# Moving the start addresses of three groups of SBUF tiles in a two-layer decoder trunk

## The chip, the cores and the metric

The kernel runs on one core of one Trainium2 chip. The metric is the device time of one execution in microseconds (us). Times of one instruction are in nanoseconds (ns); the matrix engine's clock is given in cycles where the granted clock is 1.00, its full 2.4 GHz.

## The reference, cut to what matters

The reference computes a decoder trunk of two layers on 256 tokens of width 1024, in float32. Each layer is a sum of residual steps:

```python
h = h + 0.5 * swiglu(rms_norm(h), w_gate, w_up, w_down)        # D_FF = 2816
u = rms_norm(h)
... = split_last(u @ w_in, IN_SIZES)                           # 8616 columns
h = h + (sum_i sigmoid(gate_i) * (y_i @ w_branch_i)) @ w_out   # four token mixers y_i
h = h + cross_attention(rms_norm(h), rms_norm(mem), wq, wk, wv, wo)
h = h + 0.5 * swiglu(rms_norm(h), ...)
```

and a last RMSNorm. Nearly all arithmetic is in the products of 256 tokens with weights that are read once from HBM.

## The kernel before, in words

**Three products for one.** A float32 operand is split into a high part, rounded to the matrix engine's `float32r` type, and a low part, the rest. A product is the sum of three matmuls: high by high, low by high, high by low. For weights, `fetch` does this: a DMA of up to 1 MB brings a chunk of 2048 columns into a `wr` tile, ScalarE writes the high part to a `wh` tile (L341), VectorE the rest to a `wl` tile (L342). Each of the three names has three buffers. For activations, `split` does it (L355, L356).

**Two forms of product.** TensorE first loads a stationary operand of 128 columns (LDWEIGHTS, the engine PEld of the profile) and then streams a moving operand through it (MATMUL, the engine PE). The load for the next matmul begins while the present one streams.

- `linear` (L372): the activations are stationary, 128 tokens of one 128-row block, and 512 columns of the weights move. A chunk of weights serves 24 such matmuls: two token blocks, three products, four row blocks.
- `linear_t` (L390): the weights are stationary and the 256 tokens of the activations move. A chunk serves 48.

The order of TensorE's instructions is the order of the program. Small jobs between them (transposes, attention scores) are generators that `tick` advances at fixed points.

**Where the operands come from.** The normalised residual stream, or the merged branches, lie transposed in four tiles of the pool `xp`: `xh0` and `xl0` (high and low part of the first 512 of the 1024 features) and `xh1`, `xl1` (the second 512). The class `Transposed` fills them, half by half. They are called the halves here. All other activations that meet weights (`hid` of the FFN's down projection, the mixers' outputs `y..`, the memory `mm..`, the cross attention's `xo..`, its keys `xk..`) lie in tiles of 4096 bytes of the pool `mp`. Scratch tiles of 2048 bytes (`toks`, the tag `f`, the gates) lie in the pool `fp`, between `xp` and `sp`; `sp` holds many small tiles and stands ahead of `mp`.

**Where a tile begins.** The pools stand one behind the other in a partition: `cp`, `wr`, `wh`, `wl`, `xp`, `fp`, `sp`, `mp`; within a pool, tags follow in the order of their first use, each rounded up to 32 bytes. Tiles named `gap` only take room. Sizes in the code give these starts, counted within a line of 512 bytes: the buffers of `wr`, `wh`, `wl` at 480, all four halves at 480, all tiles of `fp` at 480, all tiles of `mp` at 480. Steps within a tile from one operand to the next (512, 1024 or 2048 bytes) don't change that. Three cases differ: the weights of most `linear_t` products are written 48 elements later into their buffers (`HELD = 48`, 192 bytes), so that they begin at 160; the projection `wmisc` has 424 columns, so that its row blocks begin at 480, 128, 288 and 448 in turn; and the MLA up projections (L913) have 384, 256 and 512 columns, all beginning at 480.

**The rope tables.** `tables`, a generator, computes angles (`ang`, `angk`, `angc`, 48 elements each, two buffers each in `sp`) with some 20 short VectorE instructions during the first FFN.

Of the kernel before, what the change touches and what calls it, by code (L numbers as in the profile page):

```python
# [11 lines left out]
F32 = mybir.dt.float32  # L12
F32R = mybir.dt.float32r
# [6 lines left out]
P = 128  # L20
L = 2
D = 1024
S = 256
# [66 lines left out]
def _thresholds():  # L90
    out = list(range(1, 17))
    for k in range(1, 16):
        out.append(math.ceil(16 * 8 ** (k / 16) - 1e-9))
    return out
# [55 lines left out]
def program(tc, a, out, upto="all"):  # L150
# [4 lines left out]
    def sb(name, bufs):  # L155
        return ctx.enter_context(tc.tile_pool(name=name, bufs=bufs))
# [5 lines left out]
    xp = sb("xp", 1)  # L162
    fp = sb("fp", 2)
    sp = sb("sp", 4)
# [3 lines left out]
    ctx.enter_context(tc.manual_schedule(engines={mybir.EngineType.PE}))  # L168


    sp.tile([P, 48], F32, tag="gap", name="gap", bufs=1)

    def bank(name):
        return aux.tile([P, 512], F32, tag="aux", name=name)
# [1 line left out]
    def m4(name, dtype=F32):  # L176
        return mp.tile([P, 1024], dtype, tag="m", name=name)
# [7 lines left out]
    def f2(name, tag="f", bufs=5):  # L185
        return fp.tile([P, 512], F32, tag=tag, name=name, bufs=bufs)

    def half(name):
        return f2(name, "half", 2).rearrange("p (k t) -> p k t", k=4)

    def small(name, n):
        return sp.tile([P, n], F32, tag=name, name=name, bufs=2 if n <= 64 else 1)
# [16 lines left out]
    def C(name):  # L209
        o, n = CO[name]  # L210
        return cst[:, o - P:o - P + n]
# [5 lines left out]
    def bcol(l, name):  # L217
        o, n = BO[name]
        return bcs[:, l * NBC + o:l * NBC + o + n]
# [133 lines left out]
    def split(hi, lo, src):  # L353

        act.activation(hi, src, AF.Copy)  # L355
        dve.tensor_tensor(lo, src, hi.bitcast(F32), ALU.subtract)  # L356
# [40 lines left out]
    def transpose4(src, n=4):  # L397

        ps = bank("tr")
        for k in range(n):  # L400
            pe.transpose(ps[:, k * P:(k + 1) * P], src[:, k * P:(k + 1) * P], ident)  # L401
        return ps[:, :n * P].rearrange("p (k t) -> p k t", k=n)

    def split_gain(hi, lo, ps, gain, n=4):

        t = f2("sgt")[:, :n * P].rearrange("p (k t) -> p k t", k=n)
        dve.tensor_tensor(t, ps, gain.unsqueeze(2).to_broadcast([P, n, P]), ALU.mult)
        split(hi[:, :n], lo[:, :n], t)

    def blk(b):  # L410
        return slice(b * P, (b + 1) * P)

    def rstd_of(ss, n, m, name):

        t = small("rs" + name, m)
        r = small(name, m)
        dve.tensor_scalar(t, ss, 1.0 / n, EPS, ALU.mult, ALU.add)
        pool.tensor_tensor(r, t, mhalf[:, :m], ALU.pow)
        return r

    def square_sum(src, out_):
        j = fp.tile([P, 512], mybir.dt.bfloat16, tag="junk", name="junk", bufs=1)
        act.activation(j[:, :src.free_size()], src, AF.Square, accum_out=out_)  # L423

    class Transposed:
# [12 lines left out]
        def half(self, c, wait):  # L438
            yield wait
            hi = xp.tile([P, 4, S], F32R, tag=f"xh{c}", name=f"xh{c}")  # L440
            lo = xp.tile([P, 4, S], F32R, tag=f"xl{c}", name=f"xl{c}")
            for b in range(NB):
                ps = transpose4(self.src(b, c))
                if self.gain is None:
                    split(hi[:, :, blk(b)], lo[:, :, blk(b)], ps)
                else:
                    split_gain(hi[:, :, blk(b)], lo[:, :, blk(b)], ps, self.gain[:, c * 4:(c + 1) * 4])
            self.tiles[c] = (hi, lo)
            if self.name is not None:
                yield 1 if now > 8 else 6  # L450
                with tc.issue_after(last.ins) if now < 20 else ExitStack():
                    for b in range(NB):
                        square_sum(self.src(b, c), self.ss[:, 2 * c + b:2 * c + b + 1])
                if c:
                    s2 = small("ss2", NB)
                    dve.tensor_tensor(s2, self.ss[:, 0:2], self.ss[:, 2:4], ALU.add)
                    self.rstd = rstd_of(s2, D, NB, self.name)
# [73 lines left out]
    def tables():  # L531
        yield 10
        pos = m4("pos").bitcast(I32)
        posi, reli = pos[:, :NB + S], pos[:, 512:896]
        with tc.issue_after(last.ins):
            act.dma_start(posi, a["pos"])
            act.dma_start(cst, a["consts"][:, P:CO["dec"][0]])
            act.dma_start(bcs, a["bcols"])
        act.activation(sel, C("sel")[:16], AF.Copy)
        yield 4  # L540
        for o, b, n in ((0, 0, 128), (128, 1, 256)):
            pool.tensor_tensor(reli[:, o:o + n], posi[:, b:b + 1].to_broadcast([P, n]), posi[:, NB:NB + n], ALU.subtract)
        dve.tensor_copy(relt, reli)
        yield 2
        posf = small("posf", NB)
        dve.tensor_copy(posf, posi[:, :NB])
        twopi = 2 * math.pi
        c1 = 6.28125
        c2 = float(np.float32(np.round((twopi - c1) * 2 ** 21) / 2 ** 21))
        c3 = float(np.float32(twopi - c1 - c2))  # L550
        magic = 1.5 * 2 ** 23
        for b in range(NB):
            ang = small("ang", 48)
            k = small("angk", 48)
            dve.tensor_scalar(ang, C("inv"), posf[:, b:b + 1], None, ALU.mult)
            dve.tensor_scalar(k, ang, 1.0 / twopi, magic, ALU.mult, ALU.add)
            dve.tensor_scalar(k, k, magic, None, ALU.subtract)
            for c in (c1, c2, c3):
                dve.scalar_tensor_tensor(ang, k, -c, ang, ALU.mult, ALU.add)
            co = small("angc", 48)  # L560
            dve.tensor_scalar(co, ang, math.pi / 2, None, ALU.add)
            dve.tensor_scalar(k, co, math.pi, -twopi, ALU.is_gt, ALU.mult)
            dve.tensor_tensor(co, co, k, ALU.add)
            lim = 3.1415925
            dve.tensor_scalar(co, co, lim, -lim, ALU.min, ALU.max)
            dve.tensor_scalar(ang, ang, lim, -lim, ALU.min, ALU.max)
            for o, n, f in ((0, 32, 0), (96, 16, 32)):
                act.activation(tab[:, b, o:o + n], co[:, f:f + n], AF.Sin)
                act.activation(tab[:, b, o + n:o + 2 * n], ang[:, f:f + n], AF.Sin)
                dve.tensor_scalar(tab[:, b, o + 2 * n:o + 3 * n], tab[:, b, o + n:o + 2 * n], -1.0, None, ALU.mult)  # L570
            yield 2

        for l in range(L):
            lp = bcol(l, "lam").rearrange("p (i e d) -> p i e d", i=2, e=2)
            pr = f2("lp")[:, :128].rearrange("p (i d) -> p i d", i=2)
            dve.tensor_tensor(pr, lp[:, :, 0], lp[:, :, 1], ALU.mult)
            s2 = small("ls", 2)
            dve.tensor_reduce(s2, pr, AX.X, ALU.add)
            e2 = small("le", 2)
            act.activation(e2, s2, AF.Exp)  # L580
            li = 0.8 - 0.6 * math.exp(-0.3 * l)
            dve.tensor_tensor(nlam[:, l:l + 1], e2[:, 1:2], e2[:, 0:1], ALU.subtract)
            dve.tensor_scalar(nlam[:, l:l + 1], nlam[:, l:l + 1], li, None, ALU.subtract)

        rel = relt
        rb = bcs[:, L * NBC:].rearrange("p (h k) -> p h k", h=H)
        d8 = sp.tile([P, H, BUCKETS], F32, tag="d8", name="d8", bufs=1)
        dve.tensor_scalar(d8[:, :, 0], rb[:, :, 0], 8.0, None, ALU.mult)
        dve.tensor_tensor(d8[:, :, 1:], rb[:, :, 1:], rb[:, :, :BUCKETS - 1], ALU.subtract)
        dve.tensor_scalar(d8[:, :, 1:], d8[:, :, 1:], 8.0, None, ALU.mult)  # L590
        for hd in range(H):
            dve.tensor_copy(bias[:, hd, 0:128], C("dmask")[:, 128:256])
            dve.tensor_copy(bias[:, hd, 128:384], C("dmask"))
            dve.tensor_scalar(bias[:, hd], bias[:, hd], d8[:, hd, 0:1], None, ALU.add)
        for i, t in enumerate(_thresholds()):
            yield 3

            while 60 <= now < 72:
                yield 1
            ge = (f2("ge", "gate", 4) if now < 60 else f2("ge", "toks", 3))[:, :384]  # L600
            with tc.high_priority(-2000), tc.issue_after(paced.ins):
                dve.tensor_scalar(ge, rel, float(t), None, ALU.is_ge)
                for hd in range(H):
                    dve.scalar_tensor_tensor(bias[:, hd], ge, d8[:, hd, i + 1:i + 2], bias[:, hd], ALU.mult, ALU.add)  # L604
        mark("bias")
# [636 lines left out]
```

## Time and profile before

| | |
|---|---|
| median of three runs | 1589.47 us (1588.9 to 1590.79) |
| the profiled execution | 1589.41 us |
| its span, first to last instruction | 1587.5 us, 20810 instructions |
| TensorE busy (PE) | 1573.3 us, 99% |
| weight loads (PEld) | 1347.7 us, beside PE |
| VectorE, ScalarE | 1067.1 us (67%), 825.6 us (52%) |
| DMA | 281.58 MB, 177 GB/s in the mean |

PE counts the moving of operands, PEld the loading of stationary ones. The duration that the profile gives a matmul contains the way through the array and overlaps the next matmul's; what a matmul costs in a stream is the distance from its start to the next one's start, called its pitch here. It is read from the view of the chain in order of time, where a piece of one line with its length and count gives length by count.

### The profile page before, as it was taken

The page shows a single profiled execution, that of the slowest core. Times are in us where ns is not written, and L with a number is a line of the kernel's source. Part 1 is how long each engine was busy: PE and PEld are TensorE (multiplying, and loading weights), DVE is VectorE, ACT ScalarE, POOL GpSimd, SP SyncE. Part 2 cuts the span into 40 slices and gives each one's busy share as a digit, 9 for nine tenths or more (in the row PEclk, how much of TensorE's full clock was granted, in tenths as well). Part 3 has the DMA queues.
Part 4 walks back from the last instruction along what each step waited for, and adds up shares of the span by engine and source line. Part 5 has one row for each costly group of instructions (what it writes and reads, how often), then busy time and mean ns, then how long its engine had stood idle before and what let it go on. Part 6 is the DMA issues. An engine that isn't in the chain of part 4 may idle for free.

```text
span 1587.5 us, 20810 instructions
## 1 busy us (share of the span) xinstructions
PE 1573.3 (99%) x8236; PEld 1347.7 (85%) x8236; DVE 1067.1 (67%) x1698; ACT 825.6 (52%) x1221; POOL 28.0 (2%) x39
## 2 busy tenths in 40 slices
PE   8999999999999999999999999999999999999998
PEld 6888889898888988888888888898988899888886
DVE  6687699997777666554465546697657766565544
ACT  6544446656654545444454444475575554554443
POOL 0000000000000000000000000000000000000000
PEclk9999999999999999999999999999999999999999
DMA  7655554444555544555555556444546554455552
GB/s 290 204 174 193 188 174 160 158 163 150 209 185 167 182 157 162 185 185 175 192 191 185 186 174 211 150 153 161 184 151 207 186 182 164 156 178 179 191 175 76
DMA packets 41713, 281.58 MB, mean 177 GB/s; under 512 B 4624, under 2 KB 5008, under 8 KB 9488
## 3 DMA queue, kind: packets, MB, share of 16 engines
q1 hardware_dynamic: 39600, 275.07, 51.2%
q10 hardware_dynamic: 2016, 5.19, 1.0%
q8 instruction: 64, 1.05, 0.3%
q14 instruction: 33, 0.27, 0.0%
HBM read 279.20 MB, written 1.05 MB: 177 GB/s over the span
## 4 chain that ended last, share of the span: by engine, by line
PE 98%; ACT 0%; DMA 0%; issue 0%; DVE 0%; SPq 0%; POOLq 0%; POOL 0%
PE lin L372 78%; PE lin L390 11%; PE tr L401 2%; PE ht L507 1%; PE xo L1148 1%; PE xs L1102 1%; PE up L913 1%; PE my L829 0%; PE ds L998 0%; DMA h<-x 0%; PE ms L949 0%; PE pt L640 0%; ACT wh L341 0%; PE my L831 0%; PE do L1021 0%
## 5 line engine op out<-in xcount | busy, mean ns | idle before, releaser
L342 DVE TENSOR_TENSOR wl<-wr,wh 128x1024 fp32r<-128x1024 f32 (+2 forms) x534 | 625.3, 1196 | 383.5 <-ACT wh L341 381.2
L341 ACT ACTIVATE wh<-wr 128x1024 fp32r<-128x1024 f32 (+2 forms) x534 | 533.4, 1033 | 504.7 <-PE lin L372 382.9
L372 PE MATMUL lin<-wh,xh 128*128 128x512 f32 (+1 forms) x1216 | 333.7, 396 | 0.2 <-ACT wh L341 0.2
L372 PE MATMUL lin<-wh,xl 128*128 128x512 f32 (+1 forms) x1216 | 325.4, 389 | 0.0
L372 PE MATMUL lin<-wl,xh 128*128 128x512 f32 (+1 forms) x1216 | 324.6, 389 | 0.0
L372 PEld LDWEIGHTS lin<-wh,xl 128*128 128x128 f32 x1216 | 228.8, 188 | 47.7
L372 PEld LDWEIGHTS lin<-wl,xh 128*128 128x128 f32 x1216 | 228.4, 188 | 47.4
L372 PEld LDWEIGHTS lin<-wh,xh 128*128 128x128 f32 x1216 | 222.5, 189 | 43.1 <-ACT wh L341 1.2
L372 PE MATMUL lin<-wh,hid 128*128 128x512 f32 x704 | 176.0, 390 | 0.0
L372 PEld LDWEIGHTS lin<-wh,hid 128*128 128x128 f32 x704 | 131.6, 188 | 27.1
L372 PE MATMUL lin<-wl,hid 128*128 128x512 f32 x352 | 95.4, 389 | 0.0
L372 PEld LDWEIGHTS lin<-wl,hid 128*128 128x128 f32 x352 | 66.1, 188 | 13.8
L517 ACT ACTIVATE sg<-lin,rffn 128x256 f32<-128x256 f32 x88 | 40.9, 464 | 62.9 <-PE lin L372 62.8
L604 DVE SCALAR_TENSOR_TENSOR bias<-ge,d,bias 128x384 f32<-128x384 f32 x124 | 69.7, 616 | 0.3
L390 PE MATMUL lin<-xh,wh 128*128 128x256 f32 x384 | 62.0, 283 | 0.0
L390 PE MATMUL lin<-xh,wl 128*128 128x256 f32 x384 | 60.5, 279 | 0.0
L390 PE MATMUL lin<-xl,wh 128*128 128x256 f32 x384 | 60.5, 279 | 0.0
L518 DVE SCALAR_TENSOR_TENSOR toks<-lin,rffn,sg 128x256 f32<-128x256 f32 x88 | 42.3, 481 | 25.1 <-ACT sg L517 25.1
L390 PEld LDWEIGHTS lin<-xh,wh 128*128 128x128 f32 x384 | 52.0, 188 | 0.3
L390 PEld LDWEIGHTS lin<-xl,wh 128*128 128x128 f32 x384 | 51.7, 188 | 0.0
L390 PEld LDWEIGHTS lin<-xh,wl 128*128 128x128 f32 x384 | 51.7, 188 | 0.0
L423 ACT ACTIVATE junk<-h 128x512 bf16<-128x512 f32 x36 | 22.4, 622 | 30.5 <-DVE h L491 16.9
(385 smaller groups left out, 1537.0 us busy)
## 6 DMA issues: line engine op xcount, KB each, us to landing
wr<-gu SPq DMA_DIRECT2D x87, 1024.0 KB, 5.1
wr<-win SPq DMA_DIRECT2D x68, 1024.0 KB, 5.1
wr<-dn SPq DMA_DIRECT2D x40, 1024.0 KB, 4.9
wr<-wbr SPq DMA_DIRECT2D x16, 1024.0 KB, 4.9
wr<-w_out SPq DMA_DIRECT2D x8, 1024.0 KB, 5.0
wr<-xa_wk SPq DMA_DIRECT2D x8, 1024.0 KB, 5.0
wr<-xa_wq SPq DMA_DIRECT2D x8, 1024.0 KB, 5.0
wr<-xa_wv SPq DMA_DIRECT2D x8, 1024.0 KB, 5.0
```

What stands on the lines that cost most here:

```text
L341: last = act.activation(hi[:, s], r[:, s], AF.Copy)
L342: dve.tensor_tensor(lo[:, s], r[:, s], hi[:, s].bitcast(F32), ALU.subtract)
L372: pe.matmul(p_[b][:, :n], lhsT=xT(part, k0 + k)[:, b * P:(b + 1) * P], rhs=w[:, k * n:(k + 1) * n], start=first, stop=last)
L390: pe.matmul(ps[i][:, j * 256:(j + 1) * 256], lhsT=ws[w][:, o:o + P], rhs=xT(part, k0 + k), start=k0 + k + part + w + j == 0, stop=k0 + k = ...
L401: pe.transpose(ps[:, k * P:(k + 1) * P], src[:, k * P:(k + 1) * P], ident)
L423: act.activation(j[:, :src.free_size()], src, AF.Square, accum_out=out_)
L507: pe.transpose(ps[:, k, blk(b)], toks[:, b, k * P:(k + 1) * P], ident)
L517: act.activation(sg, ps[:, :256], AF.Silu, scale=xT.r[:, b:b + 1])
L518: paced = dve.scalar_tensor_tensor(toks[:, b], ps[:, 256:], xT.r[:, b:b + 1], sg, ALU.mult, ALU.mult)
L604: dve.scalar_tensor_tensor(bias[:, hd], ge, d8[:, hd, i + 1:i + 2], bias[:, hd], ALU.mult, ALU.add)
L913: pe.matmul(ps[:, :n], lhsT=lowT[p_][:, k0 + k, blk(b)], rhs=wm[w][:, o + k * n:o + (k + 1) * n], start=i == 0, stop=i == len(seq) - 1)
L1102: pe.matmul(ps[:, j], lhsT=q[part][:, 2 * j + k, blk(b)], rhs=kT[c][w][:, 2 * j + k], start=not part + w + k, stop=w + k == 2)
```

## The change: what it does

A gap of 112 elements (448 bytes) is put ahead of the halves in `xp`; the low part of the first half is made 32 elements (128 bytes) longer than it needs; the gap at the head of `sp` grows from 48 to 128 elements (192 to 512 bytes). To make room, the angles lose their six tiles of 192 bytes in `sp` and are taken as three slices of one 2048-byte tile of the tag `f`.

```diff
-    sp.tile([P, 48], F32, tag="gap", name="gap", bufs=1)
+    xp.tile([P, 112], F32, tag="gap", name="gap")
+    sp.tile([P, 128], F32, tag="gap", name="gap", bufs=1)
@@ Transposed.half
             hi = xp.tile([P, 4, S], F32R, tag=f"xh{c}", name=f"xh{c}")
-            lo = xp.tile([P, 4, S], F32R, tag=f"xl{c}", name=f"xl{c}")
+            lo = xp.tile([P, 4 * S + (0 if c else 32)], F32R, tag=f"xl{c}", name=f"xl{c}")
+            lo = lo[:, :4 * S].rearrange("p (k t) -> p k t", k=4)
@@ tables
         for b in range(NB):
-            ang = small("ang", 48)
-            k = small("angk", 48)
+            angs = f2("ang")
+            ang, k, co = (angs[:, i * 48:(i + 1) * 48] for i in range(3))
...
-            co = small("angc", 48)
```

No instruction is added, removed or reordered in the program. In bytes: 480 + 448 = 928, so `xh0` and `xl0` begin at 416 of a 512-byte line; 128 bytes more bring `xh1` and `xl1` to 544, that is 32; `fp` follows at 32. `sp`'s tiles before `mp` shift by 448 + 128 + 320 - 1152 = -256 bytes in all, so `mp` begins at 224. The weights stay at 480, or 160 with `HELD`.

The start of the stationary operand less that of the moving one, within 512 bytes, becomes:

| product | before | after |
|---|---|---|
| `linear` on the first half | 0 | -64 |
| `linear` on the second half | 0 | +64 |
| `linear` on `hid`, `y..`, `mm..`, `xo..` | 0 | -256 |
| `linear_t` on the first half | 192 | 256 |
| `linear_t` on the second half | 192 | 128 |
| `linear_t` on `mm..` (keys) | 192 | -64 |

## Rows read from the trace of the kernel before

**Rows 1.** The page: busy time by engine (share of the span, instructions), and of the span in 40 slices TensorE's busy tenths and its granted clock.

```profile
PE 1573.3 (99%) x8236; PEld 1347.7 (85%) x8236; DVE 1067.1 (67%) x1698; ACT 825.6 (52%) x1221; POOL 28.0 (2%) x39
...
PE   8999999999999999999999999999999999999998
...
PEclk9999999999999999999999999999999999999999
```

**Rows 2.** The waits of TensorE, all of them: what waited, for whom, us in total, times, longest.

```profile
PE tr L401 <- DMA ident<-consts: 4.5, 1, 4.5
PE tr L401 <- DMA h<-x: 1.8, 1, 1.8
PE lin L372 <- ACT wh L341: 0.2, 1, 0.2
PE ds L998 <- ACT mpA L641: 0.2, 1, 0.2
```

**Rows 3.** The groups of TensorE's matmuls by line and operands (count, then busy us and mean ns of one with its way through the array).

```profile
L372 PE MATMUL lin<-wh,xh 128*128 128x512 f32 (+1 forms) x1216 | 333.7, 396 | 0.2 <-ACT wh L341 0.2
L372 PE MATMUL lin<-wh,xl 128*128 128x512 f32 (+1 forms) x1216 | 325.4, 389 | 0.0
L372 PE MATMUL lin<-wl,xh 128*128 128x512 f32 (+1 forms) x1216 | 324.6, 389 | 0.0
L372 PE MATMUL lin<-wh,hid 128*128 128x512 f32 x704 | 176.0, 390 | 0.0
L372 PE MATMUL lin<-wl,hid 128*128 128x512 f32 x352 | 95.4, 389 | 0.0
L390 PE MATMUL lin<-xh,wh 128*128 128x256 f32 x384 | 62.0, 283 | 0.0
...
L390 PE MATMUL lin<-mmh,wh 128*128 128x256 f32 x128 | 20.4, 281 | 0.0
...
L372 PE MATMUL lin<-wh,mmh 128*128 128x512 f32 x64 | 17.6, 397 | 0.0
```

**Rows 4.** The chain of work that ended last, shares by line (page, part 4).

```profile
PE lin L372 78%; PE lin L390 11%; PE tr L401 2%; PE ht L507 1%; PE xo L1148 1%; PE xs L1102 1%; PE up L913 1%; PE my L829 0%; PE ds L998 0%; DMA h<-x 0%; PE ms L949 0%; PE pt L640 0%; ACT wh L341 0%; PE my L831 0%; PE do L1021 0%
```

**Rows 5.** The chain in order of time (start us, length us, what): three pieces of `linear`, two groups of the FFN's first projections and the down projection, with transposes between.

```profile
51.03 10.93 PE lin L372 x48
62.40 10.93 PE lin L372 x48
...
141.97 38.13 PE lin L372 x168
180.09 0.87 PE tr L401 x8
```

**Rows 6.** Timeline of TensorE in the down projection (start us, length us, engine, line, operation, count).

```profile
147.29 1.98 PE L372 MATMUL lin<-wh,hid 128*128 128x512 f32 x8
149.10 1.07 PE L372 MATMUL lin<-wl,hid 128*128 128x512 f32 x4
...
158.17 1.98 PE L372 MATMUL lin<-wh,hid 128*128 128x512 f32 x8
```

**Rows 7.** The chain in order of time: two pieces of `linear_t`, and between them the cross attention's scores (L1102), which have the same shape and both operands at 480.

```profile
508.35 19.79 PE lin L390 x168
...
545.55 2.87 PE xs L1102 x24
548.42 5.45 PE lin L390 x48
```

**Rows 8.** Timeline of TensorE inside those scores.

```profile
547.29 0.40 PE L1102 MATMUL xs<-xk0l,xq 128*128 128x256 f32 x2
547.53 0.64 PE L1102 MATMUL xs<-xk0h,xq 128*128 128x256 f32 x4
548.01 0.40 PE L1102 MATMUL xs<-xk0l,xq 128*128 128x256 f32 x2
```

**Rows 9.** The chain in order of time: 12 matmuls of 512 columns and the 48 of `wmisc` with 424 columns in one piece.

```profile
234.70 12.02 PE lin L372 x60
```

**Rows 10.** Timeline of TensorE in the MLA up projections: 384 columns, then 256; all operands at 480.

```profile
325.23 0.51 PE L913 MATMUL up<-wh,lowh 128*128 128x384 f32 x2
325.57 0.52 PE L913 MATMUL up<-wh,lowl 128*128 128x384 f32 x2
325.94 0.52 PE L913 MATMUL up<-wl,lowh 128*128 128x384 f32 x2
326.29 0.28 PE L913 MATMUL up<-wh,lowh 128*128 128x256 f32 x1
```

**Rows 11.** Busy time by engine in stretches of the down projection, of `linear_t`, of the scores and of `wmisc` (us, busy us and count by engine, granted clock, DMA share, GB/s).

```profile
147.40:163.60 16.20, 16.20 (x73) 13.41 (x72) 9.91 (x14) 5.06 (x7) 0.00 (x0) 1.00 0.60 204
528.60:545.20 16.60, 16.60 (x143) 16.60 (x143) 10.25 (x11) 7.08 (x11) 0.00 (x0) 1.00 0.53 173
546.30:548.20 1.90, 1.90 (x18) 1.90 (x17) 1.90 (x3) 0.87 (x1) 0.00 (x0) 1.00 0.45 190
237.30:246.40 9.10, 9.10 (x49) 8.87 (x48) 7.95 (x19) 4.29 (x6) 1.01 (x1) 1.00 0.35 117
```

**Rows 12.** The supply of weights: the two splitting groups (count, busy us, mean ns, idle time before them and who ended it).

```profile
L342 DVE TENSOR_TENSOR wl<-wr,wh 128x1024 fp32r<-128x1024 f32 (+2 forms) x534 | 625.3, 1196 | 383.5 <-ACT wh L341 381.2
L341 ACT ACTIVATE wh<-wr 128x1024 fp32r<-128x1024 f32 (+2 forms) x534 | 533.4, 1033 | 504.7 <-PE lin L372 382.9
```

**Rows 13.** The DMA issues of the FFN's weights, and SyncE's longest wait.

```profile
wr<-gu SPq DMA_DIRECT2D x87, 1024.0 KB, 5.1
...
SPq L334 <- DVE wl L342: 1307.7, 241, 14.9
```

**Rows 14.** The instructions on the tile `ang` (count, duration ns least/median/greatest, first and last start us).

```profile
L559 DVE SCALAR_TENSOR_TENSOR ang<-angk,ang x6: 198/200/202, 44.9 to 45.8; 128x48 f32<-128x48 f32 x6
L569 ACT ACTIVATE tab<-ang x4: 199/208/230, 47.1 to 50.4; 128x32 f32<-128x32 f32 x2, 128x16 f32<-128x16 f32 x2
```

## The prediction

> **What bounds the kernel now.** I read the page first: PE is busy for 1573.3 of 1587.5 us and the granted clock is at its full level in every slice [rows 1]. TensorE's waits come to 6.7 us, 6.3 of them for the first DMAs [rows 2], and the chain that ended last is TensorE's own, 78% `linear` (L372) and 11% `linear_t` (L390) [rows 4]. So the time is the number of matmuls by their pitch, and the change leaves the number as it is. What remains to ask is whether the pitch depends on where operands begin.
>
> The pitch of `linear`: in the down projection 48 matmuls lie between the starts at 147.29 and 158.17 us, so 10.88 / 48 = 226.7 ns [rows 6]; the whole piece gives 38.13 / 168 = 227.0 [rows 5]. At the granted 1.00 [rows 11] that is 544 cycles for 512 columns, 32 more than one column a cycle would need. Pieces that start behind transposes give 10.93 / 48 = 227.7 [rows 5]: some 50 ns are lost at each start.
>
> The pitch of `linear_t`, 256 columns, is 19.79 / 168 = 117.8 ns (282.7 cycles) in one piece and 5.45 / 48 = 113.5 (272 cycles) in another [rows 7]. The scores, the same shape, both operands at 480, take 0.72 / 6 = 120.0 ns (288 cycles) [rows 8]. So over the 106.7 ns of 256 columns there are 13.3 ns with equal starts, and 11.1 or 6.8 with the stationary operand 192 bytes on. This is the one place where the trace compares starts at one shape: equal starts are the dearest, by 2.2 or 6.5 ns. That `linear_t` has two pitches with the same starts says that history counts too.
>
> Two more rows bear on it. The 48 matmuls of `wmisc`: the piece of 60 takes 12.02 us, less 12 x 0.2267 leaves 9.30 / 48 = 193.7 ns [rows 9], that is 17.0 over the 176.7 of 424 columns. The 384 columns of the MLA projection: 1.06 / 6 = 176.7 ns [rows 10], 16.7 over 160.0. The first has unequal starts in three of four row blocks, the second equal ones; both are 3.4 to 3.7 ns worse than the 13.3 of 512 columns with equal starts.
>
> **The change part by part.** *Counts.* On the halves `linear` has 3 x 1216 matmuls [rows 3], 96 of them `wmisc`, so 3552 of 512 columns. On tiles of `mp` it has 704 + 352 = 1056 for `hid` and 3 x 64 = 192 for `mm` [rows 3], by the code 192 more for `xo` and 2 layers x 4 branches x 48 = 384 for `y`: 1824. Together 5376, or 1218.6 us at 226.7 ns. `linear_t` has 3 x 384 = 1152 on the halves and 3 x 128 = 384 on `mm` [rows 3].
>
> *The halves at -64 and +64, `mp` at -256, against the weights (`linear`).* No row shows 512 columns with these distances, so the price has bounds. Towards a gain: the least extra over the columns that any row shows is 6.8 ns (the 113.5 ns piece), against 13.3 now; 6.5 ns by 5376 is 35 us. Towards a loss: the dearest are 16.7 and 17.0; 3.7 ns by 5376 is 20 us. Between them I take the row that is nearest in kind, the same shape with starts apart, in the state that it is in for most of its length: 120.0 - 117.8 = 2.2 ns less. By 5376 that is -11.9 us.
>
> *`linear_t`: distances of 256, 128 and -64 in place of 192.* They are unequal before and after. Bounds: all 1536 at 113.5 gives -4.3 x 1536 = -6.6 us, all at 120.0 gives +2.2 x 1536 = +3.4 us. I take 0, since nothing in the rows ranks one unequal distance over another.
>
> *The scores and the cross attention's products with V* change little: L1102 and L1148 are 1% of the chain each [rows 4], and 6.5 ns on 120 would be 5% of that, under 1 us each. I take 0.
>
> *The starts behind transposes.* About 50 ns each; a hundred of them are 5 us. Whether other starts lengthen or shorten them no row tells: 0, and 5 us either way for the range.
>
> *The angles in one tile of the tag `f`.* The same instructions of 0.2 us run from 41 to 50 us [rows 14]. VectorE and ScalarE have hundreds of us of idle time, and what ScalarE waits for there is TensorE [rows 12]. A later start would delay the rope tables, which are first read by the mixers, behind 220 us; the five buffers of `f` turn over in that time. 0; with the cover gone it would be the 9 us of that stretch, which I leave out.
>
> *The other engines.* `fp` and `mp` move for VectorE and ScalarE as well. They have 33% and 48% of the span free [rows 1], so even 5% longer instructions stay beside TensorE.
>
> *The supply.* A chunk lasts 24 matmuls, 5.44 us. At 13.3 ns less per matmul it would last 5.1. The DMA takes 5.1 us to land [rows 13], but there are three buffers, and its queue waits mostly for a raw buffer to be split [rows 13]; ScalarE's 382.9 us before the split are waits for TensorE to give a buffer back [rows 12]. So TensorE sets the pace of the supply, with two halves of 1.03 and 1.20 us to make per chunk. Cost 0.
>
> *Sum.* Against the profiled execution's own 1589.4 us (its span is 1.9 less; the median of the runs shown is 1589.5): 1589.4 - 11.9 = 1577.5 us, 0.7% faster.
>
> *A rule weighed against the rows.* The Trainium skill, "TensorE: Matmul & The Clock Gate", section "Step-by-step: what each phase is for", says that TensorE has two independent read ports on SBUF, and: "Loading the next tile's weights doesn't steal SBUF read bandwidth from the running matmul." By it the starts would not matter and the sum would be 1589.4. The rows agree with it in so far as loads run beside the streams [rows 11], and speak against it in that one shape has three pitches [rows 7, 8].
>
> **The rivals.** *No change.* The extra may belong to the moving stream alone: 32 cycles on 512 columns and 16 on 256 (the 113.5 ns piece) are both one in sixteen, as if each 64 bytes of the stream cost a cycle. Then `linear` is already at its floor, and only `linear_t` can move, within -6.6 and +3.4 us. For it: the ratio fits both shapes, and the pitch of `linear` is the same in all long pieces. Against it: 288 cycles with equal starts. Time 1589. The Trainium skill's rule on the two ports, named above, would have it so.
>
> *A large gain.* Starts apart free `linear` to the least extra seen, 6.5 ns on all 5376: 1589.4 - 35 = 1554. On the halves alone it is 23 us, 1566. For it: such a piece exists in `linear_t`; against it: it is the rarer of the two states there.
>
> *Slower.* With equal starts, load and stream keep step and settle at 544 cycles; with starts apart they don't settle and every matmul pays what `wmisc` pays, 3.7 ns more, because the distance of the two readers passes through collisions at other times. The place is `linear`; on all of it 1589.4 + 20 = 1609, on the halves alone 1603. It decides once the mean pitch of `linear` is over 227.3 ns, as 0.6 x 5376 is the 3.2 us that a measurement can tell. For it: the pitch right behind transposes, before it settles, is above 226.7, and the only unequal starts in `linear` today are the dear ones. Against it: the 384 columns are as dear with equal starts, so that the dearness may come from a length other than 512 columns.
>
> *The change doesn't do what it says.* The starts follow from sizes alone, and the tiles named `gap` take their room before too; I leave this without a chance of its own.
>
> **How the numbers follow.** About 0.2% is what a measurement of this kernel can tell from no change, 3.2 us. Small gain, as forecast: 0.40. Large gain, 1567 and below: 0.14. No change: 0.21. Slower: 0.25. So faster 0.54, same 0.21, slower 0.25. The likeliest is 1577.5; its own range is 1568 to 1586. For 8 in 10 the range must take in no change, most of the slower case and about half of the large gains: the loss's far end, 1609, less the 1 to 3 us by which not every product would pay it, and the gain's far end 1554: 1554 to 1607.
>
> **What would show it.** The profile of the changed kernel should have the same counts in every group, granted clock 1.00 and no new wait of TensorE. In the chain, the pieces of 48 and 168 of `linear` should take 10.8 and 37.8 us in place of 10.93 and 38.13. If the halves and `mp` behave differently, the pieces of 48 and those of 168 part. `linear_t`'s piece of 168 should stay within 19.1 to 20.2. The prediction is wrong if the pieces of `linear` keep 226.7 ns (no change), fall to 220 (large gain) or rise to 230 (slower), or if a wait for ScalarE's `wh` appears among TensorE's waits.

## The result: 1.0% slower, and the profile after

The changed kernel takes 1606.32 us (median; 1605.84 to 1606.78) against 1590.03 (1588.9 to 1590.79) for the kernel before on the same chip: ratio 1.0104, 95% interval 1.0091 to 1.0116. That is 16.3 us slower where 11.9 us faster was forecast. The range's upper end lies 0.7 us above the result. Of the rivals, *Slower* came true, and nearly at the figure that it gave for the halves alone, 1603.

The page of the changed kernel, busy time by engine and the granted clock:

```profile
PE 1590.3 (99%) x8236; PEld 1350.3 (84%) x8236; DVE 1068.1 (67%) x1698; ACT 829.7 (52%) x1224; POOL 27.8 (2%) x39
...
PEclk9999999999999999999999999999999999999999
```

TensorE has the same 8236 instructions as in [rows 1] and is busy 17.0 us longer, at the same granted clock. ScalarE has three more, loads of its tables (34 against 31, 1.28 us each), though the program adds none; that is most of the 4.1 us that it is busy longer. All waits of TensorE (what waited, for whom, us in total, times, longest):

```profile
PE tr L403 <- DMA ident<-consts: 4.5, 1, 4.5
PE tr L403 <- DMA h<-x: 2.2, 1, 2.2
PE lin L374 <- ACT wh L343: 0.2, 1, 0.2
PE ds L1000 <- ACT mpA L643: 0.2, 1, 0.2
```

Against [rows 2] 0.4 us are new, in a DMA at the very beginning. So neither the clock, nor the supply, nor a wait explains 16 us: the same matmuls take longer. Which ones, the groups tell (count, then busy us and mean ns of one with its way through the array):

```profile
L374 PE MATMUL lin<-wh,xh 128*128 128x512 f32 (+1 forms) x1216 | 337.8, 399 | 0.2 <-ACT wh L343 0.2
L374 PE MATMUL lin<-wh,xl 128*128 128x512 f32 (+1 forms) x1216 | 330.2, 393 | 0.0
L374 PE MATMUL lin<-wl,xh 128*128 128x512 f32 (+1 forms) x1216 | 330.0, 393 | 0.0
L374 PE MATMUL lin<-wh,hid 128*128 128x512 f32 x704 | 176.1, 390 | 0.0
L374 PE MATMUL lin<-wl,hid 128*128 128x512 f32 x352 | 95.4, 389 | 0.0
L392 PE MATMUL lin<-xh,wh 128*128 128x256 f32 x384 | 62.9, 286 | 0.0
L392 PE MATMUL lin<-mmh,wh 128*128 128x256 f32 x128 | 20.4, 281 | 0.0
```

Beside [rows 3]: the three groups on the halves are 3 to 4 ns longer each, `linear_t` on the halves 3 ns; `hid` and `mm`, which both moved by 256 bytes, stand where they stood. The chain in order of time (start us, length us, what) says the same in pitches:

```profile
52.36 11.10 PE lin L374 x48
63.90 11.10 PE lin L374 x48
...
144.65 38.13 PE lin L374 x168
...
514.83 19.79 PE lin L392 x168
535.07 17.20 PE lin L392 x144
...
555.01 5.69 PE lin L392 x48
```

On the halves 48 matmuls take 11.10 us, 231.3 ns each, where they took 10.93 [rows 5]. The down projection's 168 take 38.13 us as before, to the hundredth. `linear_t` on `mm` keeps its 19.79 us, while the 48 that follow the scores, on the second half, went from 5.45 [rows 7] to 5.69.

The timeline of TensorE in the first of these pieces (start us, length us, operation, count) parts the halves. The first 24 matmuls are on the second half, +64 bytes off, the others on the first, -64:

```profile
55.00 1.09 PE L374 MATMUL lin<-wh,xh 128*128 128x512 f32 x4
...
57.80 1.09 PE L374 MATMUL lin<-wh,xh 128*128 128x512 f32 x4
...
62.39 1.08 PE L374 MATMUL lin<-wl,xh 128*128 128x512 f32 x4
```

From 55.00 to 57.80 there are 12 matmuls: 233.3 ns each, 560 cycles. From 57.80 to 62.39 there are 20: 229.5 ns, 551 cycles. Before, all settled at 226.7, 544 cycles.

These means are not scatter. Taken one by one, the starts in the trace show fixed sequences: on the first half the distances 226, 229 and 232 ns repeat, on the second 231 and 236. Leaving out the first ten and the last of each stretch, 99% and 100% of the matmuls agree within 1 ns with the one three, or two, places before. Nor do the other engines' accesses to memory explain it: on the second half the mean is 233.3 ns beside a VectorE that is busy for over 95% of the matmul and 233.5 beside one that is idle for as much.

Adding up, over the whole trace, the distance from each matmul's start to the next one's start, by operand, gives the bill:

| TensorE's instructions | before, us | after, us | change |
|---|---|---|---|
| `linear`, 512 columns, first half | 408.18 | 413.02 | +4.84 |
| `linear`, 512 columns, second half | 409.59 | 419.07 | +9.48 |
| `linear` on `hid` | 240.08 | 240.19 | +0.11 |
| `linear` on `y..`, `mm..`, `xo..` | 175.94 | 176.22 | +0.28 |
| `linear_t` on the first half | 68.51 | 69.65 | +1.14 |
| `linear_t` on the second half | 67.91 | 69.37 | +1.45 |
| `linear_t` on `mm..` | 45.40 | 45.40 | 0.00 |

Together +17.3 us, the growth of the span from 1587.5 to 1604.8. 83% of it is `linear` on the halves. `wmisc` and all else come to zero. The first half's figure is blurred: at the head of the kernel, up to about 12 us, some of its matmuls take about 427 ns each, not equally many in every run. Runs in which `linear` has the distances of before (e1, e5, e7, e11, e12) differ in it by -0.6 to +1.1 us, nearly all of it there; of the +4.84 here, 0.43 lie in the first 48 matmuls.

### The profile page after: what moved, and what is told of

It is laid out like the page before. It is cut to its first block, busy times and chain, and to the rows that moved or that the text cites. A ratio compares the mean times of both kernels' runs of the same rounds, so it can differ in the third digit from the quotient of the medians.

```text
span 1604.8 us, 20813 instructions
## 1 busy us (share of the span) xinstructions
PE 1590.3 (99%) x8236; PEld 1350.3 (84%) x8236; DVE 1068.1 (67%) x1698; ACT 829.7 (52%) x1224; POOL 27.8 (2%) x39
## 4 chain that ended last, share of the span: by engine, by line
PE 98%; ACT 0%; DMA 0%; issue 0%; DVE 0%; SPq 0%; POOLq 0%; POOL 0%
PE lin L374 78%; PE lin L392 11%; PE tr L403 2%; PE ht L510 1%; PE xo L1150 1%; PE xs L1104 1%; PE up L915 1%; PE my L831 0%; PE ds L1000 0%; DMA h<-x 0%; PE ms L951 0%; PE pt L642 0%; ACT wh L343 0%; PE my L833 0%; PE do L1023 0%
## 5 line engine op out<-in xcount | busy, mean ns | idle before, releaser
L374 PE MATMUL lin<-wh,xh 128*128 128x512 f32 (+1 forms) x1216 | 337.8, 399 | 0.2 <-ACT wh L343 0.2
L374 PE MATMUL lin<-wh,xl 128*128 128x512 f32 (+1 forms) x1216 | 330.2, 393 | 0.0
L374 PE MATMUL lin<-wl,xh 128*128 128x512 f32 (+1 forms) x1216 | 330.0, 393 | 0.0
```

The costliest lines, as they stand in the source:

```text
L374: pe.matmul(p_[b][:, :n], lhsT=xT(part, k0 + k)[:, b * P:(b + 1) * P], rhs=w[:, k * n:(k + 1) * n], start=first, stop=last)
```

## The experiments

Two readings stood against each other. **Distance:** the pitch of a matmul depends on where its stationary operand begins relative to its moving one, and 64 bytes either way lose a rhythm that equal starts had. **Something else that moved:** the angles, the scratch tiles in `fp`, the tiles of `mp`, or the place of an operand in the line as such. A third question, which the prediction's term rested on, is whether the time above one column a cycle is a collision of the stream with the loads.

What an experiment did to a class of matmuls is told below as the change of its sum of start-to-start distances against the kernel before, as in the table above. Ratios are to the kernel before on the same chip with their 95% intervals; where none is given, the kernel was timed once.

### e1: the angles alone

The changed kernel with all starts put back to 480.

```diff
-    xp.tile([P, 112], F32, tag="gap", name="gap")
-    sp.tile([P, 128], F32, tag="gap", name="gap", bufs=1)
+    sp.tile([P, 336], F32, tag="gap", name="gap", bufs=1)
...
-            lo = xp.tile([P, 4 * S + (0 if c else 32)], F32R, tag=f"xl{c}", name=f"xl{c}")
+            lo = xp.tile([P, 4 * S + (0 if c else 0)], F32R, tag=f"xl{c}", name=f"xl{c}")
```

> The angles lie in slices of one scratch tile as in the changed kernel, but the gaps are chosen so that all starts are those of before (halves, scratch and activations at 480). Theory 'starts': the time of before, 1589.5 us within 2, and the pitches of before (linear 226.7 ns, linear_t 117.8). Rival 'angles': the move of the angles delays something, and a part of the 16 us shows here.

1589.41 us, ratio 0.9999 (0.999 to 1.0008). Its chain, a piece on the halves:

```profile
51.58 10.93 PE lin L373 x48
```

The pitch of before. The rope tables' new tile costs nothing that can be seen; the loss lies in the starts.

### e2 and e3: one half at a time

Only the first half at 416 (distance -64), everything else at 480:

```diff
-    sp.tile([P, 128], F32, tag="gap", name="gap", bufs=1)
+    sp.tile([P, 208], F32, tag="gap", name="gap", bufs=1)
...
-            lo = xp.tile([P, 4 * S + (0 if c else 32)], F32R, tag=f"xl{c}", name=f"xl{c}")
+            lo = xp.tile([P, 4 * S + (0 if c else 16)], F32R, tag=f"xl{c}", name=f"xl{c}")
```

> Only the first half of the tokens' tiles is moved, 64 bytes less than the weights; the second half, the scratch and the activations start as before. Theory 'each product pays by its own distance': the products on the first half lost 4.8 us in linear and 1.1 us in linear_t in the changed kernel, and lose the same here: 1595.5 us, the second half's products as before. Rival 'the alternation of two different starts costs': the second half's products lose as well, and the time is nearer 1606 than 1595.

Only the second half at 32 (distance +64):

```diff
-    xp.tile([P, 112], F32, tag="gap", name="gap")
-    sp.tile([P, 128], F32, tag="gap", name="gap", bufs=1)
+    sp.tile([P, 208], F32, tag="gap", name="gap", bufs=1)
...
-            lo = xp.tile([P, 4 * S + (0 if c else 32)], F32R, tag=f"xl{c}", name=f"xl{c}")
+            lo = xp.tile([P, 4 * S + (112 if c else 16)], F32R, tag=f"xl{c}", name=f"xl{c}")
```

> Only the second half is moved, 64 bytes more than the weights; all else starts as before. Theory 'own distance': its products lost 9.5 us in linear and 1.5 us in linear_t in the changed kernel: 1600.5 us here, the first half as before. Rival 'alternation': the first half's products lose too.

The first half alone: 1595.03 us, ratio 1.0032 (1.0019 to 1.0045); `linear` on that half +3.42 us, on the untouched one +0.30, `linear_t` on that half +1.19, on the untouched one +0.43. The second half alone: 1603.34 us, ratio 1.0085 (1.0068 to 1.0101); `linear` on that half +10.08, `linear_t` on it +1.44, and `linear` on the untouched first half +2.46. So e2 came out nearly as 'own distance' said, and e3 did not: 2.8 us more than its 1600.5, as the rival had it that the other half loses too. The timeline of e3 shows what the last figure is. The second half's 24 matmuls end at 57.86, then come the first half's, with equal starts:

```profile
55.06 1.09 PE L373 MATMUL lin<-wh,xh 128*128 128x512 f32 x4
...
57.86 1.09 PE L373 MATMUL lin<-wh,xh 128*128 128x512 f32 x4
58.79 1.08 PE L373 MATMUL lin<-wh,xl 128*128 128x512 f32 x4
59.71 1.07 PE L373 MATMUL lin<-wl,xh 128*128 128x512 f32 x4
...
62.43 1.07 PE L373 MATMUL lin<-wl,xh 128*128 128x512 f32 x4
```

From 55.06 to 57.86, 12 at 233.3 ns. Then 8 in 1.85 us, 231 ns each, and from 59.71 on 12 in 2.72 us: 226.7, the settled pitch. So a stream with equal starts comes back to 544 cycles, but needs about eight matmuls for it, while the half that is 64 bytes off never gets there. That is part of why the parts do not simply add: +5.3 and +13.6 us alone, +16.3 together. In the changed kernel the first half does not come back to 544 cycles anyway, so there is nothing of that to lose; by the sums of the traces this half accounts for 1.0 us of the difference, the second half for 0.9, the rest lies outside `linear`.

### e4, e5 and e10: other distances

To see whether the loss grows with distance, whether a better one exists, and whether it repeats: the first half at 128, the second at 32, `mp` at -32 (e4); both halves at -256 (e5); the first at 96, the second at 160 (e10). Against the changed kernel, e4:

```diff
-    xp.tile([P, 112], F32, tag="gap", name="gap")
-    sp.tile([P, 128], F32, tag="gap", name="gap", bufs=1)
+    xp.tile([P, 32], F32, tag="gap", name="gap")
+    sp.tile([P, 72], F32, tag="gap", name="gap", bufs=1)
...
-            lo = xp.tile([P, 4 * S + (0 if c else 32)], F32R, tag=f"xl{c}", name=f"xl{c}")
+            lo = xp.tile([P, 4 * S + (120 if c else 104)], F32R, tag=f"xl{c}", name=f"xl{c}")
```

In e5 these three numbers are 64, 208 and `(64 if c else 0)`, in e10 24, 208 and `(88 if c else 16)`.

> A look at three distances that no kernel has had: first half 128 bytes more than the weights, second half 32 bytes more, activations 32 bytes less. Theory 'own distance, repeating every 256 bytes': each group of products has one pitch of its own; linear_t on the first half now has a distance of 64 (as the cross attention's two products had in the changed kernel, 113 to 118 ns) and should fall under 120; linear at 128 is between 226 and 237 ns. If only whole 64-byte pieces count, 32 bytes either way give 226.7 as before; if the byte distance itself counts, 32 either way leave 226.7, to opposite sides or to the same.

> Both halves are moved 256 bytes less than the weights, all else starts as before. Theory 'the two readers meet again every 256 bytes': linear's distance of 256 is as good as 0, and linear_t's of 192 + 256 as good as 192, so the time is that of before, 1589.5 us within 3, with 226.7 ns in linear's long pieces and 117.8 in linear_t. Rival 'only equal starts settle, and the activations at -256 were spared for another reason': the halves pay as in the changed kernel, 1605 us or more.

> A look at linear's last distances: first half 96 bytes more than the weights, second half 160 bytes more, all else as before. So far linear settles at 226.7 ns with 0 and 256, and takes 229 to 234 with 32, 64, 128, 192 and 224. Theory 'only whole periods of 256 keep step': 229 to 235 ns here too. Rival 'some distance is better than 0': under 226 ns for one of the two. linear_t on the first half has 96 and gives the 119.7 ns of the earlier look if the byte distance alone counts.

e4: 1619.38 us. e10: 1612.44 us, timed once each. e5: 1590.0 us, ratio 1.0001 (0.9992 to 1.001). The chain of e4, a piece on the halves and the down projection, whose tiles are now 32 bytes off:

```profile
52.42 11.16 PE lin L374 x48
...
145.28 39.20 PE lin L374 x168
```

The chain of e10, a piece on the halves:

```profile
51.83 11.22 PE lin L374 x48
```

The chain of e5, the same piece:

```profile
50.62 10.93 PE lin L374 x48
```

The down projection, deaf to -256 in the changed kernel, goes to 39.20 / 168 = 233.3 ns with -32. And the halves, 231 ns with 64 off, are back at 10.93 us per 48 with -256. The distance therefore counts within 256 bytes, not within 512 as the table ahead of the prediction has it. And 32 bytes either way cost about as much as 64, so it is not whole pieces of 64 bytes that count. Put together, by the change of each class over its number of matmuls (1776 for a half, 1056 for `hid`), starts behind transposes included:

| distance, within 256 bytes | ns per matmul of 512 columns against equal starts | from |
|---|---|---|
| 0 | +0.1, -0.3, 0.0 | `hid` of the changed kernel, first and second half of e5 (all at -256) |
| 32 | +5.1 | e4, second half |
| 64 | +5.3, +5.7 | changed kernel and e3, second half |
| 96 | +6.8 | e10, first half |
| 128 | +5.5 | e4, first half |
| 160 | +5.3 | e10, second half |
| 192 | +2.7, +1.9 | changed kernel and e2, first half |
| 224 | +6.3 | e4, `hid` |

Equal starts, and equal starts plus 256, are the best of the eight places; -64 (192) is the mildest of the others. No order by distance is seen beyond that. Entries of the first half carry the blur told above, up to 0.6 ns; without the first 48 matmuls the -0.3 is 0.0. An entry also depends on the neighbour: 192 costs +1.9 beside a half with equal starts and +2.7 beside one that is 64 off. e4 and e10 were each timed once, but their excess of 30 and 23 us is nine times or more the spread of the runs of the kernel before. On `linear_t` e10 missed what it expected: at 96 the first half stayed at 119.0 ns, not 119.7.

### e11 and e12: the same distances in another place

Every buffer from `wr` on moved by +64 bytes, to 32 of a line (e11), or by -32, to 448 (e12); among these buffers the distances are those of before. What lies in `cp` ahead of them stays, also `ident`, an operand of the transposes.

```diff
-    cp.tile([P, 8], F32, tag="gap0", name="gap0")
+    cp.tile([P, 24], F32, tag="gap0", name="gap0")
...
-    sp.tile([P, 48], F32, tag="gap", name="gap", bufs=1)
+    sp.tile([P, 208], F32, tag="gap", name="gap", bufs=1)
```

That is e11 against the kernel before, which apart from this has the angles in `f` as the changed kernel has; e12 is the kernel before without the line of `gap0`.

> Weights, halves, scratch and activations are all moved by 64 bytes together, so that they begin at 32 of a 512-byte line, and every distance is that of before. Theory 'distance': the time of before, 1589.5 us within 2. Rival 'the place in the line': the second half began at 32 in the changed kernel and lost most; then linear loses here as well, up to 30 us.

> Weights, halves, scratch and activations all begin 32 bytes less, at 448, which is a multiple of 64; every distance is that of before. Theory 'the stream pays one cycle in sixteen by itself, wherever it begins': 1589.5 us within 2, linear at 226.7 ns. Rival 'the cycle in sixteen is paid for starts in the middle of a 64-byte piece': linear falls towards 213 ns, up to 65 us less.

1590.22 us, ratio 1.0003 (0.9993 to 1.0012), and 1590.01, ratio 1.0002 (0.9992 to 1.0012). Chain of e11, a piece on the halves:

```profile
62.94 10.94 PE lin L373 x48
```

Chain of e12, the same piece:

```profile
63.17 10.93 PE lin L371 x48
```

For `linear` the place in the line does not count, only the distance of the two operands. For `linear_t` that much is not shown: on the second half it takes 0.83 (e11) and 0.82 us (e12) more at the same distance, as its pieces that ran at 113.3 ns run at 117.8 here.

### e6 and e7: the distance of `linear_t`

In the kernel before, `HELD = 48` keeps the weights of `linear_t` 192 bytes from the activations. e6 makes that 64. e7 spreads it over the products: 32, 96, 224 and 128 bytes.

```diff
-HELD = 48
+HELD = 16
```

```diff
-                yield from chunks([win[l, g]], KD, 512, HELD)
+                yield from chunks([win[l, g]], KD, 512, 8)
...
-                yield from chunks([win[l, g]], KD, 512, HELD)
+                yield from chunks([win[l, g]], KD, 512, 24)
...
-                    yield from chunks([a[n][l, c]], KD, 512, 0 if n == "xa_wv" else HELD)
+                    yield from chunks([a[n][l, c]], KD, 512, {"xa_wk": 56, "xa_wq": 32, "xa_wv": 0}[n])
```

> The kernel before with the weights of linear_t 64 bytes into their buffers in place of 192: linear_t's distance is 64, nothing else moves. Theory 'own distance': linear_t falls from 117.8 to the 115.6 ns that the first half showed at 64 in the scan, on 1536 matmuls: 3.4 us less, 1586 us; 1583 if it settles at 113.3 throughout. Rival: the gain at 64 came from the moved x tiles themselves, and the time stays at 1589.5.

> A look at other distances of linear_t, with all activations at 480: 32 bytes for the convolution's products, 96 for the differential attention's, 224 for the cross attention's keys, 128 for its queries. From the changed kernel and the scan, ns by distance: 0 120.0, 64 115.6, 128 118.9, 160 120, 192 117.8, 224 116.7. Theory 'own distance': 128 gives 118.9 and 224 gives 116.7 again; 32 and 96 lie between 113.3 and 121.

e6: 1586.63 us, ratio 0.9982 (0.9973 to 0.9991), the fastest kernel of this study; `linear_t` on `mm` -1.45 us, on the first half -1.18, on the second -0.52. e7: 1591.66 us; -0.05, +0.35, +1.15. The chain of e6 in the stretch of [rows 7]:

```profile
507.67 19.07 PE lin L390 x168
527.18 16.96 PE lin L390 x144
...
547.02 5.65 PE lin L390 x48
```

The 168 on `mm` take 113.5 ns each where they took 117.8, but the 48 behind the scores rose from 113.5 to 117.7. The same shape with the same starts still has two pitches, 113.3 and 117.8, and 64 bytes make the lower one more frequent. What selects between them is not shown; what ran before is a guess. e6 came out as its theory said (1586 us), and its rival, that the time stays, is out. The other four distances of e7 give means from 118 to 120, starts behind other work included. Behind these, by the trace, its pieces run at 118.3 ns (32), 117.4 or 118.8 (96), 116.6 or 117.8 (224) and 118.6 (128). 32 and 96 lie where they were expected, 128 near its 118.9, 224 only in part at its 116.7: it is not one pitch per distance.

### e8 and e9: a shorter load

With equal starts the load of 128 columns takes 188 ns of the 226.7. If the stream loses its 13.3 ns to the load, a load that reads half or a sixteenth should give them back. In the down projection of the kernel before, all but the first and last matmuls of a bank load and compute 64 (e8) or 8 (e9) of the 128 stationary columns; the sums of the other tokens are left out. The edit is that of e8; e9 has 8 in place of 64.

```diff
-                            pe.matmul(p_[b][:, :n], lhsT=xT(part, k0 + k)[:, b * P:(b + 1) * P],
+                            m_ = 64 if kt == KF and not first and not last else P
+                            pe.matmul(p_[b][:m_, :n], lhsT=xT(part, k0 + k)[:, b * P:b * P + m_],
```

> The kernel before, but in the down projections all matmuls except the first and the last of each sum load 64 stationary columns in place of 128, so that half of the tokens' sums are left out; the 512 moving columns stay. Theory 'the load takes the extra from the stream': with half of the load the 13.3 ns over 512 columns become about 7, and the pieces of 168 take 36.9 us or less. Rival 'the moving stream pays one cycle in sixteen by itself': 226.7 ns, 38.1 us as before.

> As with half a load, but 8 stationary columns in place of 128 in the down projections' middle matmuls (most of their sums are left out); 512 columns move. Half a load gave 552 cycles in the mean, neither of what the two theories had said. Theory 'the stream pays one cycle in sixteen by itself, and collisions with the load come on top (8 with half a load, 0 where load and stream keep step)': hardly any load, so 544 cycles, 226.7 ns, and no scatter. Rival 'all 32 cycles are the load's': 512 to 520 cycles, 213 to 217 ns.

1592.13 and 1592.62 us: nothing gained, `linear` on `hid` 3.1 us dearer in both. The groups of loads of e9 (count, busy us and mean ns of one): a full one, and the tiny ones.

```profile
L373 PEld LDWEIGHTS lin<-wh,xl 128*128 128x128 f32 x1216 | 228.8, 188 | 47.7
...
L373 PEld LDWEIGHTS lin<-wl,hid 128*8 128x8 f32 x352 | 32.6, 93 | 49.7
```

The chain of e8, the first down projection:

```profile
141.58 38.65 PE lin L373 x168
```

The chain of e9, the first and a later one:

```profile
141.95 38.10 PE lin L373 x168
...
740.40 38.84 PE lin L373 x168
```

The loads did become short, 93 ns against 188 (136 in e8), and the stream did not become faster. With 64 columns the pitch is 230.1 ns. With 8 columns one piece holds 226.8 and another, with the same instructions and the same starts, takes 231.2. Neither reading had this: the load's length is not what the 13.3 ns are made of, and a shorter load can disturb a stream that a full one leaves settled. The other pieces of the trace say more. In the kernel before, all seven pieces of the down projections that begin behind transposes are at 226.7 ns from about the tenth matmul on. With 8 columns one of the seven gets there, the first shown, and six run near 231; the four pieces that continue a settled stream stay at 226.7. With 64 columns even these four leave it, for 230. So the load is not the price of the settled stream, but it has a part in whether a stream comes back to it. In no run was a long piece of 512 columns below 226.7 ns.

## Why the prediction was wrong, step by step

**What bounds the kernel** was right: the time is the number of `linear` and `linear_t` matmuls by their pitch, with the granted clock at its full level and no new waits to speak of. So was that the counts stay. The prediction's test, that pieces of 48 and of 168 part if the halves and `mp` behave differently, is what happened.

**The term that failed** is the one of `linear`, -2.2 ns by 5376. On the 3552 on the halves the measured change is +14.32 us, +4.0 ns each; on the 1824 of `mp` it is +0.39 us, nothing. It failed in its sign, not only in its size, and the step that failed is the transfer from one shape to another. The price was taken from one comparison, 120.0 against 117.8 ns at 256 columns [rows 7, 8], read as "equal starts are the dearest", and put on 512 columns. There equal starts are the best of the eight places tried. The reading behind it, that the 13.3 ns are what load and stream lose to each other, fails as well: e9 leaves 8 of 128 columns of the load, and the 13.3 ns stay.

For 256 columns the row was right, and the changed kernel confirms it. The first scores' queries lie in `fp`, at 32, and their keys in `mp`, at 224, which is 64 within 256 bytes where it was 0. The table ahead of the prediction leaves them out. Their timeline, and the chain at a piece of `linear_t` on the first half, which is now at 0 within 256:

```profile
552.58 0.39 PE L1104 MATMUL xs<-xk0l,xq 128*128 128x256 f32 x2
...
554.62 0.39 PE L1104 MATMUL xs<-xk0l,xq 128*128 128x256 f32 x2
```

```profile
334.00 5.75 PE lin L392 x48
```

The scores ran at 2.04 / 18 = 113.3 ns where they took 120.0, and `linear_t` at 5.75 / 48 = 119.8 where it took 117.8. At 256 columns equal starts are thus among the dearest, with 160 (120.0 in e4); at 512 columns they are the best. Why the two shapes differ in sign no run shows.

**`mp` at -256** was counted as starts apart. It is no change: the distance repeats after 256 bytes (`hid` here, e5 on the halves). No row shown of before tells that.

**`linear_t` at 0** was off by +2.6 us, inside its bound of +3.4. "Nothing ranks one unequal distance over another" was a fair reading of the rows; e6 shows that there is a rank, with 64 bytes the best of those tried. And the first half's 256 was not one more unequal distance but 0: the scores' own row would have priced it at 576 x 2.2 = 1.3 us, and 1.14 were measured.

**The angles, the scores, the other engines and the supply at 0** hold: e1 for the angles; the first scores' piece is 0.13 us shorter (2.74 against 2.87 [rows 7]); VectorE and ScalarE are busy 1.0 and 4.1 us longer, off the path; no wait for `wh` was added.

**The rivals.** *Slower* had the place (`linear` on the halves) and nearly the price: 3.7 ns from `wmisc`, 4.0 measured. That the prices agree is luck: 4.0 is the mean of 2.7 and 5.3, and `wmisc` itself, whose distances changed as well, did not move (-0.03 us). Its mechanism holds in part: with equal starts a stream settles at 544 cycles (e3, from the ninth matmul on), and with starts apart it does not; but what it does instead is to repeat a dearer sequence, not to stay irregular. That this comes of the load's reading was not shown; e8 and e9 show only that, with equal starts, a shorter load keeps most pieces from settling too. *No change* was right in so far as no run went below 544 cycles, one more in sixteen, and wrong that nothing comes on top of it. *Large gain* found no row in any run.

**The rule on the two read ports** of the Trainium skill ("TensorE: Matmul & The Clock Gate", section "Step-by-step: what each phase is for"), by which loads take nothing from the stream, does not tell the whole. The trace of e9 agrees with it in so far as a load of 93 ns in place of 188 gave the stream nothing back. That the starts would not matter, which the prediction took from it, does not hold: the same loads and streams cost 16.3 us more or less by where they begin relative to each other. The prediction doubted the rule because one shape has several pitches, which was sound, and drew the wrong sign for `linear` from it.

**Where the chances should have been.** The rows of before held one warning of the right sign: a `linear` stream that is not settled, behind transposes, is dearer than a settled one [rows 5]. `wmisc`'s dear row [rows 9] looked like a second warning, but it is as dear after the change. The row that was believed was of another shape in another function, and no row of before had 512 columns with starts apart; the chances for a gain and a loss should have been closer to even.

**What stays open.** Why a stream settles at 544 cycles or repeats a dearer sequence, why the distance repeats after 256 bytes, and why 512 and 256 columns differ in sign, no run here tells. Nor is it known what selects the two pitches of `linear_t`.

## What to carry to other kernels

When two operands of the same stream of matmuls lie in tiles whose starts are set by the sizes of other tiles, compare the pitch of long pieces in the trace before moving anything: here a stationary operand that begins 0 or 256 bytes from the moving one ran at 226.7 ns, and seven other distances in steps of 32 bytes at 229 to 234. Take the price of such a move from rows of the very shape, and from several distances; a neighbouring shape can have the other sign (for 256 columns equal starts were among the dearest, and for `linear_t` 64 bytes were better than 192, worth 0.18%). A small unrelated tile added to a pool can make such a move unnoticed.

## What the runs showed of the hardware that was not expected

- The distance of the starts of the two operands changes the pitch of 512 columns from 226.7 ns to 229 to 234; 256 bytes count as 0, and the place in the line does not matter for it (e11, e12).
- A stream with starts apart is not irregular: it repeats a short sequence, 226, 229, 232 ns at -64 bytes and 231, 236 ns at +64.
- For 256 columns equal starts are among the dearest: the same scores ran at 120.0 ns with 0 and at 113.3 with 64.
- A stream hands its state on: in e3 the half with equal starts needs about eight matmuls (231 ns) to come back to 226.7, +2.46 us in all.
- Shortening the load from 188 to 93 ns gave no faster stream, and with 8 stationary columns two pieces of the same 168 matmuls took 38.10 and 38.84 us: six of seven pieces behind transposes no longer came back to 226.7 ns, where with 128 columns all seven did.
- Matmuls of 256 columns at a distance of 192 or 64 run at 113.3 or 117.8 ns, a whole piece in the one or the other but for its first matmuls.
